# Seven half-size products in place of eight in a feed-forward down projection

## The chip, the cores and the metric

The kernel runs on one core of one Trainium2 chip. Its metric is the device time in microseconds. Three runs of the kernel before gave 2230.1 us in the median (2228.79 to 2231.28). TensorE, VectorE, ScalarE and GpSimd each have their own in-order queue of instructions and wait for each other by semaphores; SyncE issues the DMAs that load weights.

## The reference

The reference is two transformer blocks on 512 tokens of width 1024 in float32: attention, a gated delta rule and a mixture of experts, then a second block with an mLSTM, a short convolution and stick-breaking attention. The change touches only the second block's feed-forward part, whose width is 4096, and what follows it:

```
h2 = rmsnorm(x, norm_mlp_g)
x = x + square(relu(h2 @ w_up)) @ w_down      # w_up 1024x4096, w_down 4096x1024
return rmsnorm(x, norm_final_g)
```

## The kernel before, in words

Every dense product is computed in fp32r with a split: each operand is the sum of a high half (a rounded copy, made by a cast on ScalarE) and a low half (the rest, made by a subtraction on VectorE), and three matmuls, high x high and the two mixed ones, stand for one product.

Dense work is a list of jobs (`add_job`, L157). A job has a piece of weights of 128x1024 numbers, half of a 1 MB load. The loads go through a ring of two buffers (`ringA`, L2167), `get` takes a loaded one, and `release` frees it and issues the next load (L132 to L139). `presplit` (L167) makes the high and low half of the weights into one of three `hl` buffers, two jobs ahead of the job that runs (`run_jobs`, L197, `look=2`). Then the job's matmuls are issued and its result is taken out of PSUM.

The up projection uses `fm` (L234): each load gives two jobs of 24 matmuls (8 blocks of the contraction x 3 terms) that write the 128 hidden units of the job for all 512 tokens into one PSUM bank. `ev_up` (L2152) takes it out: relu on ScalarE, square on VectorE, then the high and low halves of the result into `uT`, which has one buffer per quarter of the hidden width, two in turn. The down projection uses `tm` (L287): for one quarter (1024 hidden units) and one half of the 1024 output columns (`nh`), four jobs of 24 matmuls add into four PSUM banks, one for each 128 tokens, and `ev_res` (L2131) adds each bank to `x1`, the residual stream in SBUF, on VectorE. The very last half goes through `tm_whole` (L319), which finishes one token block after the other, so that the final norm of a block can run beside the matmuls of the next. The loop at L1689 interleaves: up of quarter 0, then up of quarter q+1 and down of quarter q.

In this stage six PSUM banks serve the accumulators (`pacc3`) and two a pool `psm3`, which only the norm ahead of the stage uses (L1795). The order of instructions within an engine's queue is written when the program is built, by a list scheduler that goes by its own model of durations and by program order; it is not changed at run time. GpSimd has no work in the feed-forward stage but four tiny operations of the final norm.

Of the kernel before, what the change touches and what calls it, by code (L numbers as in the profile page):

```python
# [10 lines left out]
F32 = mybir.dt.float32  # L11
F32R = mybir.dt.float32r
# [3 lines left out]
AF = mybir.ActivationFunctionType  # L16
OP = mybir.AluOpType
# [9 lines left out]
def drain(g):  # L27
    for _ in g:
        pass
# [52 lines left out]
class Kern:  # L82
# [84 lines left out]
    def presplit(self, upto):  # L167
        while self.jsplit < min(upto, self.jlimit):
            j = self.jobs[self.jsplit]
            if j[3] != "second":  # L170
                self.cur_raw = self.get()
            ring, raw = self.cur_raw
            src = j[0](raw)
            if j[1] == "fm":
                hl = self.hlp.tile([128, 2, 8, 128], F32R, name="hl_fm", tag="hl")
            elif j[1] == "whole":
                hi, lo = hl = j[5]()
            elif j[1] == "tm":
# [108 lines left out]
    def tm(self, src, c0, evac, hsrc, rows=1024, r0=0, k0=0, close=True):  # L287

        st = {}
        nu = rows // 512  # L290
        for u in range(nu):
            self.ld_tm(src, r0 + u * 512, c0)
            for m in range(2):
                def view(raw, m=m):
                    return raw.rearrange("p (k c) -> p k c", k=4)[:, 2 * m:2 * m + 2, :]

                def mm(hl, u=u, m=m):
                    h = hsrc()
                    first, last = (u == 0 and m == 0), (u == nu - 1 and m == 1)
                    if first:  # L300
                        st["ps"] = [self.pacc.tile([128, 512], F32, name="acc", tag=self.atag)
                                    for _ in range(4)]
                    for c in range(4):
                        ps = st["ps"][c]
                        n = 0
                        for kk in range(2):
                            k = k0 + u * 4 + m * 2 + kk
                            for a, b in ((0, 0), (1, 0), (0, 1)):
                                self.TE.matmul(ps, h[:, a, k, c * 128:(c + 1) * 128], hl[:, b, kk, :],  # L309
                                               start=(first and n == 0), stop=(last and n == 5))  # L310
                                n += 1
                        self.step += 1
                        if last:
                            evac(c, ps)
                        self.catch_up(False)
                        yield 1.3
                self.add_job(view, "tm", mm, "first" if m == 0 else "second")

    def tm_whole(self, src, c0, evac, hsrc, tile, r0=0):  # L319

# [1323 lines left out]
    def b2_loads(self):  # L1644
        A = self.A
# [27 lines left out]
        self.tm_whole(A["w_out_2"], 512, lambda c, ps: self.ev_mid(c, ps), lambda: self.yM,  # L1673
                      lambda: self.sc.tile([128, 2, 8, 512], F32R, name="whole", tag="yB"))

        def up(q):
            for j in range(4):
                self.fm(A["w_up_2"], 1024 * q + 256 * j,
                        [lambda ps, q=q, j=2 * j + m: self.ev_up(q, j, ps) for m in range(2)], lambda: self.hT4)

        def down(q):
            for nh in range(2):
                if q == 3 and nh == 1:
                    self.tm_whole(A["w_down_2"], 512, lambda c, ps: self.ev_res(c, 1, ps, True), lambda: self.uT[3],
                                  lambda: self.b2.tile([128, 2, 8, 512], F32R, name="whole", tag="hT"), r0=1024 * q)
                else:
                    self.tm(A["w_down_2"], nh * 512, lambda c, ps, nh=nh: self.ev_res(c, nh, ps),
                            lambda q=q: self.uT[q], r0=1024 * q)
        up(0)  # L1689
        for q in range(4):  # L1690
            if q < 3:
                up(q + 1)
            down(q)

    def split_y(self, y, src, j):

# [53 lines left out]
    def second_block(self):  # L1750
        tc, A = self.tc, self.A
# [59 lines left out]
        with tc.tile_pool(name="mlp", bufs=1, reuse_waits="tile") as mp:  # L1811
            self.mp = mp
            gf = mp.tile([128, 1024], F32, name="gf")
            self.GE.dma_start(gf, self.bcast_rows(A["norm_final_g_2"], 1024))
            self.gf = gf
            self.uT = {}
            drain(first)
            drain(self.run_jobs(55))
            drain(self.tail())
        PN.__exit__(None, None, None)  # L1820
        PC.__exit__(None, None, None)
# [327 lines left out]
        next(g)  # L2149
        self.defer(lambda: drain(g), 4)  # L2150

    def ev_up(self, q, j, ps):  # L2152
        mp = self.mp
        if j == 0:
            self.uT[q] = mp.tile([128, 2, 8, 512], F32R, name="uT", tag="uT", bufs=2)
        r = mp.tile([128, 512], F32, name="up_r", tag="up_r", bufs=2)
        self.SE.activation(r, ps, AF.Relu)
        self.VE.tensor_mul(r, r, r)
        self.split_y(self.uT[q], r, j)


@with_exitstack
# [47 lines left out]
```

## Time and profile before

| | |
|---|---|
| median of the runs | 2230.1 us |
| the profiled execution | 2224.39 us |
| its span, first to last instruction | 2222.6 us |
| mean granted TensorE clock | 0.989 of full speed |
| TensorE busy in the span | 94% |
| feed-forward stage | 1863 to 2213 us of the span |

The profile's busy times count an instruction from its start to its end, waits for a shared resource within it included. The granted clock is in parts of full speed, 1.00 for 2.4 GHz and 0.50 for 1.2 GHz. The rows on which the prediction rests stand in a section of their own below.

### The profile page before, as it was taken

How to read it: one execution, taken by the hardware profiler on the slowest of the kernel's cores; microseconds unless marked ns; L12 is line 12 of the kernel's file. 1: busy time of each engine (PE TensorE's matmuls, PEld its weight loads, DVE VectorE, ACT ScalarE, POOL GpSimd, SP SyncE). 2: the span in 40 equal slices, each digit the busy share in tenths (PEclk: the TensorE clock that was granted, in tenths of full speed). 3: DMA queues.
4: the chain of work that ended last, by engine and by line, in shares of the span. 5: the costliest groups of instructions: out<-in, count | busy, mean ns of one | idle time of the engine just before them, and what ended most of it. 6: DMA issues, size and time to landing. Idle time of an engine off the chain costs nothing.

```text
span 2222.6 us, 28293 instructions
## 1 busy us (share of the span) xinstructions
PE 2092.1 (94%) x11741; PEld 1610.7 (72%) x11741; DVE 1016.1 (46%) x1635; ACT 756.4 (34%) x1181; POOL 175.8 (8%) x202
## 2 busy tenths in 40 slices
PE   6989999999888888889999999999999999999998
PEld 4767787755444444468888888888888888888886
DVE  5579667521111113555555345555454444434433
ACT  3645543311111011036666234445222343323221
POOL 1020001011111110021221000000000000000000
PEclk9999999999999999989999999999999999999999
DMA  6212101999999999811121232222333232332322
GB/s 192 76 57 76 59 2 31 362 388 417 418 416 408 405 405 397 342 59 57 58 63 56 91 92 76 73 72 82 109 96 95 95 118 82 95 95 95 95 95 76
DMA packets 161431, 354.25 MB, mean 159 GB/s; under 512 B 16678, under 2 KB 116111, under 8 KB 136723
## 3 DMA queue, kind: packets, MB, share of 16 engines
q1 hardware_dynamic: 151395, 339.24, 42.0%
q0 software_dynamic: 8480, 7.91, 1.0%
q10 hardware_dynamic: 1424, 5.24, 0.6%
q8 instruction: 94, 1.54, 0.3%
q14 instruction: 38, 0.31, 0.0%
HBM read 352.86 MB, written 22.02 MB: 169 GB/s over the span
## 4 chain that ended last, share of the span: by engine, by line
PE 55%; DVE 1%; ACT 0%; issue 0%; DMA 0%; POOLq 0%; ACTq 0%
PE acc L259 38%; PE acc L309 8%; PE acc L336 2%; PE acc L218 2%; PE sb_o L1941 1%; PE sb_z L1922 1%; PE ml_s L2063 1%; PE ml_pn L2083 1%; PE pv L1840 0%; PE sb_z L1881 0%; PE sb_z L1926 0%; PE n_ps L447 0%; PE sb_z L1888 0%; PE ml_pd L2083 0%; PE sb_z L1930 0%
## 5 line engine op out<-in xcount | busy, mean ns | idle before, releaser
L259 PE MATMUL acc<-hT,hl_fm 128*128 128x512 f32 x3504 | 822.1, 393 | 2.1 <-DVE hl_fm L165 2.0
L259 PEld LDWEIGHTS acc<-hT,hl_fm 128*128 128x128 f32 x3504 | 655.0, 189 | 140.7 <-issue 3.8
L165 DVE TENSOR_TENSOR hl_fm<-rawA,hl_fm 128x1024 fp32r<-128x1024 f32 x174 | 215.4, 1238 | 139.9 <-ACT hl_fm L161 139.8
L161 ACT CAST hl_fm<-rawA 128x1024 fp32r<-128x1024 f32 x176 | 184.7, 1049 | 267.5 <-PE acc L259 199.4
L309 PE MATMUL acc<-hl_tm,uT 128*128 128x512 f32 x672 | 152.8, 389 | 0.0
L309 PEld LDWEIGHTS acc<-hl_tm,uT 128*128 128x128 f32 x672 | 126.1, 188 | 26.2
L1448 PE MATMUL gu<-rawB,XT 128*64 128x256 f32 x992 | 130.9, 382 | 13.5 <-DMA rawB<-in_expert_w_gate_dram 13.5
L1448 PEld LDWEIGHTS gu<-rawB,XT 128*64 128x64 f32 x992 | 83.7, 137 | 49.8 <-DMA rawB<-in_expert_w_gate_dram 17.2
L1480 ACT ACTIVATE obs<-dn_o,slots 128x512 f32<-128x512 f32 x52 | 35.8, 688 | 234.3 <-PE dn_o L1477 234.3
L1437 DVE TENSOR_TENSOR XT<-g_ps,g 128x512 f32<-128x512 f32 x64 | 41.6, 686 | 143.8 <-PE g_ps L1431 143.0
L165 DVE TENSOR_TENSOR hl_tm<-rawA,hl_tm 128x1024 fp32r<-128x1024 f32 x48 | 58.7, 1224 | 66.4 <-ACT hl_tm L161 66.3
L259 PE MATMUL acc<-yA,hl_fm 128*128 128x512 f32 x384 | 87.4, 389 | 0.0
L259 PEld LDWEIGHTS acc<-yA,hl_fm 128*128 128x128 f32 x384 | 72.1, 188 | 14.9
L161 ACT CAST hl_tm<-rawA 128x1024 fp32r<-128x1024 f32 x48 | 50.3, 1048 | 93.0 <-PE acc L309 84.5
L1477 PE MATMUL dn_o<-rawB,ht 128*64 128x512 f32 x256 | 73.4, 600 | 8.8 <-DVE ht L1463 6.7
L1448 PE MATMUL gu<-rawC,XT 128*64 128x256 f32 x448 | 68.8, 386 | 6.5 <-DMA rawC<-in_expert_w_gate_dram 6.5
L309 PE MATMUL acc<-hl_tm,hT 128*128 128x512 f32 x288 | 72.4, 404 | 0.0
L1448 PE MATMUL gu<-rawH,XT 128*64 128x256 f32 x352 | 60.0, 401 | 11.0 <-DMA rawH<-in_expert_w_gate_dram 11.0
L1463 DVE COPY ht<-h_ps 128x256 f32<-128x256 f32 x32 | 13.6, 424 | 123.3 <-PE h_ps L1461 123.3
L1452 ACT ACTIVATE sg<-gu 128x256 f32<-128x256 f32 x32 | 12.3, 384 | 149.9 <-PE gu L1448 149.9
L309 PEld LDWEIGHTS acc<-hl_tm,hT 128*128 128x128 f32 x288 | 54.3, 194 | 10.9
L1454 DVE TENSOR_TENSOR hd<-sg,gu 128x256 f32<-128x256 f32 x32 | 13.4, 420 | 100.2 <-ACT sg L1452 100.2
(513 smaller groups left out, 2905.0 us busy)
## 6 DMA issues: line engine op xcount, KB each, us to landing
rawA<-in_w_in_dram SPq DMA_DIRECT2D x66, 1024.0 KB
rawB<-in_expert_w_up_dram SPq DMA_DIRECT2D x33, 1024.0 KB
rawB<-in_expert_w_down_dram SPq DMA_DIRECT2D x32, 1024.0 KB
rawB<-in_expert_w_gate_dram SPq DMA_DIRECT2D x29, 1024.0 KB
rawC<-in_expert_w_down_dram SPq DMA_DIRECT2D x16, 1024.0 KB
rawA<-in_w_up_dram SPq DMA_DIRECT2D x16, 1024.0 KB
rawA<-in_w_down_dram SPq DMA_DIRECT2D x16, 1024.0 KB
rawC<-in_expert_w_gate_dram SPq DMA_DIRECT2D x14, 1024.0 KB
```

Of the source, the lines that this page charges most:

```text
L161: self.SE.copy(hi, src)
L165: self.VE.tensor_sub(lo, src, hi.bitcast(F32))
L218: self.TE.matmul(p[:, t:t + 256], j[4][:, a, k, :], h[:, b, k, t:t + 256], start=(t == 0 and i == 0), stop=(t > 0 and i == 23), skip_group ...
L259: self.TE.matmul(ps, hl[:, a, k, :], h[:, b, k, :], start=(n == 0), stop=(n == 23))
L309: self.TE.matmul(ps, h[:, a, k, c * 128:(c + 1) * 128], hl[:, b, kk, :], start=(first and n == 0), stop=(last and n == 5))
L336: self.TE.matmul(ps, h[:, a, k, c * 128:(c + 1) * 128], st["w"][:, b, k, :], start=(n == 0), stop=(n == 23))
L1437: self.VE.tensor_tensor(xt[:, 4 * b:4 * b + 4, :], ps, self.g2[:, 4 * b:4 * b + 4, None].to_broadcast([128, 4, 128]), op=OP.mult)
L1448: TE.matmul(pg[64 * e:64 * e + 64, m * 256:(m + 1) * 256], xt[:, k, 64 * e:64 * e + 64], w[2 * m + e][:, k * 256:(k + 1) * 256], start=(m ...
L1477: TE.matmul(po[64 * e:64 * e + 64, :], ht[:, j, 64 * e:64 * e + 64], w[e].rearrange("p (j c) -> p j c", j=2)[:, j, s], start=(j == 0), sto ...
L1480: SE.activation(ob[:, s], po, AF.Copy, scale=sl[:, 1:2])
L1922: TE.matmul(z[e][b][:, c:c + n], self.ntri, hl[:, a, f:f + n], start=False, stop=(i == 3 and a == 1), skip_group_check=True)
L1941: TE.matmul(po[o, 512 - n:512], v[:, i, o], aa[e][:, self.FLAT[i]:self.FLAT[i] + n], start=(i == 0), stop=(i == 3))
```

## The change

The first three quarters of the hidden width (3072 of 4096) are cut into six chunks of 512. In a chunk, the down product is 512 tokens x 512 hidden units times 512 x 1024 weights. It is treated as a 2x2 block product (halves of the tokens, of the hidden units, of the output columns) and computed with seven block products in place of eight, by the Winograd form of Strassen's scheme: four operands are plain blocks, the others are sums of blocks.

On the weight side, `seven` takes both 1 MB loads of a chunk at once and makes P5 = W12 - W11, P6 = W22 - P5, P7 = W22 - W12 (in place) and later P4 = W21 - P6 on GpSimd; the seven jobs, in the order P1, P6, P2, P5, P7, P3, P4, have 12 matmuls each. The high halves are casts on ScalarE as before; the low halves of P6, P7 and P4 are subtractions on GpSimd, the other four on VectorE. On the token side, `ev_forms` writes seven forms for each pair of hidden blocks: relu on ScalarE, square on GpSimd, four sums of 256 columns on VectorE, and high and low halves of all. On the result side, `sums` gives pairs of PSUM banks: P2 adds into the banks of P1, P3 into those of P5, P4 into those of P7, in each case after the first result has been read out by VectorE; P6 adds over all six chunks in the two banks of `psm3`. P1 is summed into an SBUF tile `g_sum`, which, with P6 added, is added to three of the four blocks of `x1` at the end, on GpSimd. The last quarter runs as before: eight up jobs, then `tm` and `tm_whole`.

```diff
@@ presplit
+            if j[1] == "seven":
+                j[4] = j[0]()
+                self.jsplit += 1
+                continue
@@ new
+    SEVEN = (("P1", 0), ("P6", 4), ("P2", 1), ("P5", 3), ("P7", 5), ("P3", 6), ("P4", 2))
+    def seven(self, src, r0, forms, st, evac):
+        VE, SE, GE = self.VE, self.SE, self.GE
+        for nh in range(2):
+            self.ld_tm(src, r0, nh * 512)
...
+        def part(name):
+            if name == "P1":
+                w["raw"] = [self.get() for _ in range(2)]
+                w["P1"], w["P2"] = halves(w["raw"][0][1])
+                w12, w["P3"] = halves(w["raw"][1][1])
+                w["P5"] = self.mp.tile([128, 2, 512], F32, name="w_t1", tag="w_t1")
+                w["P6"] = w["P4"] = self.mp.tile([128, 2, 512], F32, name="w_t2", tag="w_t2")
+                GE.tensor_tensor(w["P5"], w12, w["P1"], op=OP.subtract)
+                GE.tensor_tensor(w["P6"], w["P3"], w["P5"], op=OP.subtract)
+                GE.tensor_tensor(w12, w["P3"], w12, op=OP.subtract)
+                w["P7"] = w12
+            hl = self.hlp.tile([128, 2, 2, 512], F32R, name="hl_tm", tag="hl")
+            x = w[name]
+            SE.copy(hl[:, 0], x)
+            if name in ("P6", "P7", "P4"):
+                GE.tensor_tensor(hl[:, 1], x, hl[:, 0].bitcast(F32), op=OP.subtract)
+            else:
+                VE.tensor_sub(hl[:, 1], x, hl[:, 0].bitcast(F32))
+            if name == "P2":
+                GE.tensor_tensor(w["P4"], x, w["P4"], op=OP.subtract)
+            if name in ("P2", "P3"):
+                self.release(w["raw"][name == "P3"][0])
+            return hl
+        def mm(hl, name, f):
+            u = forms()
+            ps, start, stop = st(name)
+            for r in range(2):
+                n = 0
+                for k in range(2):
+                    for a, b in ((0, 0), (1, 0), (0, 1)):
+                        self.TE.matmul(ps[r], u[:, f, a, k, r * 128:(r + 1) * 128], hl[:, b, k, :],
+                                       start=(start and n == 0), stop=(stop and n == 5), skip_group_check=True)
...
+            evac(name, ps)
...
+    def sums(self, c, n):
+        def st(name):
+            if name == "P6":
+                if c == 0:
+                    self.p6 = [self.psm.tile([128, 512], F32, name="p6", tag="ps") for _ in range(2)]
+                return self.p6, c == 0, c == n - 1
+            b = dict(P2="P1", P3="P5", P4="P7").get(name, name)
+            if b == name:
+                banks[b] = [self.pacc.tile([128, 512], F32, name="acc", tag=self.atag) for _ in range(2)]
+            return banks[b], b == name, b != name
+        def add(t, nh, ps):
+            for r in range(2):
+                x = self.x1[:, 2 * t + r, nh * 512:nh * 512 + 512]
+                VE.tensor_add(x, ps[r], x)
...
+            if name == "P1":
+                for r in range(2):
+                    if c == 0:
+                        VE.tensor_copy(g[:, r], ps[r])
+                    else:
+                        VE.tensor_add(g[:, r], ps[r], g[:, r])
...
+                    for t, nh in ((0, 1), (1, 0), (1, 1)):
+                        x = self.x1[:, 2 * t:2 * t + 2, nh * 512:nh * 512 + 512]
+                        GE.tensor_tensor(x, x, g, op=OP.add)
@@ b2_loads
-        up(0)
-        for q in range(4):
-            if q < 3:
-                up(q + 1)
-            down(q)
+        n = 6
+        for c in range(n):
+            up(512 * c, 2, lambda j, ps, c=c: self.ev_forms(c, j, ps))
+            if c:
+                self.seven(A["w_down_2"], 512 * (c - 1), lambda c=c - 1: self.uF[c], *self.sums(c - 1, n))
+        up(512 * n, 4, lambda j, ps: self.ev_up(j, ps))
+        self.seven(A["w_down_2"], 512 * (n - 1), lambda: self.uF[n - 1], *self.sums(n - 1, n))
+        self.tm(A["w_down_2"], 0, lambda c, ps: self.ev_res(c, 0, ps), lambda: self.uT, r0=512 * n)
+        self.tm_whole(A["w_down_2"], 512, lambda c, ps: self.ev_res(c, 1, ps, True), lambda: self.uT,
+                      lambda: self.b2.tile([128, 2, 8, 512], F32R, name="whole", tag="hT"), r0=512 * n)
@@ new
+    def ev_forms(self, c, j, ps):
...
+        r = self.ur[j] = mp.tile([128, 512], F32, name="up_r", tag="up_r", bufs=4)
+        SE.activation(r, ps, AF.Relu)
+        self.GE.tensor_tensor(r, r, r, op=OP.mult)
+        if j < 2:
+            return
+        u, k = self.uF[c], j - 2
+        a1, a2, b1, b2 = (self.ur[i][:, h * 256:h * 256 + 256] for i in (j - 2, j) for h in range(2))
+        d = mp.tile([128, 4, 256], F32, name="up_s", tag="up_s", bufs=2)
+        VE.tensor_add(d[:, 0], a2, b2)
+        VE.tensor_sub(d[:, 1], d[:, 0], a1)
+        VE.tensor_sub(d[:, 2], a1, a2)
+        VE.tensor_sub(d[:, 3], b1, d[:, 1])
+        for f, x in ((slice(0, 1), a1[:, None, :]), (slice(1, 3), r.rearrange("p (h t) -> p h t", h=2)), (slice(3, 7), d)):
+            SE.copy(u[:, f, 0, k, :], x)
+            VE.tensor_sub(u[:, f, 1, k, :], x, u[:, f, 0, k, :].bitcast(F32))
```

## Rows read from the trace of the kernel before

**Rows 1.** The page, busy time, share of the span and instructions of each engine.
```profile
PE 2092.1 (94%) x11741; PEld 1610.7 (72%) x11741; DVE 1016.1 (46%) x1635; ACT 756.4 (34%) x1181; POOL 175.8 (8%) x202
```

**Rows 2.** Chain that ended last, 1850 us on: start us, us, engine, line.
```profile
1952.32 43.52 PE acc L309 x192
...
2191.68 21.77 PE acc L336 x96
```

**Rows 3.** Table by stretch, one up and one down quarter; its columns are the first row.
```profile
core 0: us, PE busy (x) PEld busy (x) DVE busy (x) ACT busy (x) POOL busy (x), PEclk, DMA share, GB/s
...
1995.80:2039.40 43.60, 43.60 (x194) 36.10 (x193) 19.55 (x23) 15.43 (x22) 0.00 (x0) 1.00 0.29 95
2039.40:2082.90 43.50, 43.50 (x193) 36.03 (x192) 15.56 (x17) 9.44 (x10) 0.00 (x0) 1.00 0.31 99
```

**Rows 4.** Groups by line, 1880 us on: busy us, mean ns, idle before.
```profile
L165 DVE TENSOR_TENSOR hl_tm<-rawA,hl_tm 128x1024 fp32r<-128x1024 f32 x28 | 34.3, 1225 | 59.4 <-ACT hl_tm L161 59.4
L161 ACT CAST hl_tm<-rawA 128x1024 fp32r<-128x1024 f32 x28 | 29.4, 1051 | 76.0 <-PE acc L309 76.0
...
L1698 DVE TENSOR_TENSOR uT<-up_r,uT 128x512 fp32r<-128x512 f32 x32 | 21.9, 684 | 0.7 <-ACT uT L1697 0.7
L2133 DVE TENSOR_TENSOR x<-acc,x 128x512 f32<-128x512 f32 x32 | 21.5, 688 | 20.8 <-PE acc L309 12.1 <-PE acc L336 8.7
L2158 DVE TENSOR_TENSOR up_r<-up_r 128x512 f32<-128x512 f32 x31 | 21.5, 693 | 78.5 <-ACT up_r L2157 78.5
...
L2157 ACT ACTIVATE up_r<-acc 128x512 f32<-128x512 f32 x31 | 18.6, 598 | 98.3 <-PE acc L259 98.3
```

**Rows 5.** Groups by line on GpSimd, whole span.
```profile
L2096 POOL TENSOR_TENSOR ml_P<-ml_P 128x512 f32<-128x512 f32 x4 | 5.2, 1297 | 298.6 <-ACT ml_P L2095 298.6
...
L163 POOL TENSOR_TENSOR hl_fm<-rawA,hl_fm 128x1024 fp32r<-128x1024 f32 x2 | 4.7, 2353 | 0.6 <-ACT hl_fm L161 0.6
```

**Rows 6.** Groups by line on VectorE, whole span: a 256-wide subtraction.
```profile
L165 DVE TENSOR_TENSOR ml_Ps<-ml_P,ml_Ps 128x256 fp32r<-128x256 f32 x4 | 1.7, 426 | 1.9 <-ACT ml_Ps L161 1.9
```

**Rows 7.** Timeline around 965 us: start us, us, engine, line, operation.
```profile
964.96 2.35 POOL L163 TENSOR_TENSOR hl_fm<-rawA,hl_fm 128x1024 fp32r<-128x1024 f32 x1 [0.59 <-ACT hl_fm L161]
...
965.14 3.25 DVE L442 SCALAR_TENSOR_TENSOR n_xn<-x,rs_n,g_mix 128x1024 f32<-128x1024 f32 x1
...
968.31 1.27 DVE L451 TENSOR_TENSOR hT<-n_ps,hT 128x512 fp32r<-128x512 f32 x2
...
968.77 2.35 POOL L163 TENSOR_TENSOR hl_fm<-rawA,hl_fm 128x1024 fp32r<-128x1024 f32 x1
```

**Rows 8.** Groups by line on VectorE, whole span: the norm operation of rows 7 elsewhere.
```profile
L442 DVE SCALAR_TENSOR_TENSOR n_xn<-x,rs_n,g_mlp 128x1024 f32<-128x1024 f32 x4 | 5.1, 1283 | 2.7 <-POOL rs_n L424 2.7
```

**Rows 9.** Timelines of GpSimd and of VectorE around 993 us.
```profile
992.13 0.61 POOL L1865 CAST sb_K<-sb_k 64x512 fp32r<-64x512 f32 x1 [18.47 <-ACT sb_k L1834]
992.80 2.27 POOL L1866 CAST sb_K<-sb_k 64x512 fp32r<-64x512 f32 x1
...
992.77 0.69 DVE L1868 TENSOR_TENSOR sb_Kl<-sb_k,sb_K 64x512 fp32r<-64x512 f32 x1 [1.53 <-POOL sb_K L1865]
993.38 1.21 DVE L165 TENSOR_TENSOR hl_fm<-rawA,hl_fm 128x1024 fp32r<-128x1024 f32 x1
```

**Rows 10.** Timeline of the tail: two weight loads issued, the casts that waited for them.
```profile
2166.86 10.18 SPq L152 DMA_DIRECT2D rawA<-in_w_down_dram  x2
...
2173.20 2.00 ACT L161 CAST whole<-rawA 128x1024 fp32r<-128x1024 f32 x2 [2.19 <-DMA rawA<-in_w_down_dram]
...
2181.56 2.00 ACT L161 CAST whole<-rawA 128x1024 fp32r<-128x1024 f32 x2 [5.11 <-DMA rawA<-in_w_down_dram]
```

**Rows 11.** Timeline of TensorE and table by stretch around 968 us.
```profile
968.44 1.97 PE L447 MATMUL n_ps<-ident,n_xn 128*128 128x128 f32 x8 [3.34 <-DVE n_xn L442]
...
965.00:970.00 5.00, 1.66 (x9) 1.56 (x8) 4.59 (x5) 2.20 (x4) 5.00 (x3) 0.71 0.00 0
970.00:972.00 2.00, 1.85 (x8) 1.34 (x8) 1.62 (x3) 1.73 (x5) 1.12 (x1) 0.50 0.00 0
```

More of the change, by code (lines that the diff above doesn't have):

```diff
@@ L317, in tm, with halves @@
                 self.add_job(view, "tm", mm, "first" if m == 0 else "second")
+    SEVEN = (("P1", 0), ("P6", 4), ("P2", 1), ("P5", 3), ("P7", 5), ("P3", 6), ("P4", 2))
[3 more added lines that the diff above has]
+            self.ld_tm(src, r0, nh * 512)
+        w = {}
+        def halves(t):
+            v = t.rearrange("p (k c) -> p k c", k=4)
+            return v[:, 0:2, :], v[:, 2:4, :]
+        def part(name):
[30 more added lines that the diff above has]
+                                       start=(start and n == 0), stop=(stop and n == 5), skip_group_check=True)
+                        n += 1
+                self.step += 1
+                self.catch_up(False)
+                yield 1.3
+            evac(name, ps)
+        for name, f in self.SEVEN:
+            self.jobs.append([lambda name=name: part(name), "seven",
+                              lambda hl, name=name, f=f: mm(hl, name, f), "only", None, None])
@@ new lines, in sums, with evac @@
+    def sums(self, c, n):
+        VE, GE = self.VE, self.GE
+        banks = {}
+        def st(name):
[11 more added lines that the diff above has]
+                VE.tensor_add(x, ps[r], x)
+        def evac(name, ps):
+            g = self.mp.tile([128, 2, 512], F32, name="g_sum", tag="g_sum") if c == 0 and name == "P1" else None
+            if g is not None:
+                self.gsum = g
+            g = self.gsum
+            if name == "P1":
[4 more added lines that the diff above has]
+                        VE.tensor_add(g[:, r], ps[r], g[:, r])
+            elif name == "P2":
+                add(0, 0, ps)
+            elif name in ("P5", "P7"):
+                add(1, 1, ps)
+            elif name == "P3":
+                add(0, 1, ps)
+            elif name == "P4":
+                add(1, 0, ps)
+                if c == n - 1:
+                    for r in range(2):
+                        VE.tensor_add(g[:, r], self.p6[r], g[:, r])
+                    for t, nh in ((0, 1), (1, 0), (1, 1)):
+                        x = self.x1[:, 2 * t:2 * t + 2, nh * 512:nh * 512 + 512]
+                        GE.tensor_tensor(x, x, g, op=OP.add)
+        return st, evac
@@ L1674, in b2_loads, with up @@
                       lambda: self.sc.tile([128, 2, 8, 512], F32R, name="whole", tag="yB"))
[L1676 to L1688, printed above, removed]
-        up(0)
-        for q in range(4):
-            if q < 3:
-                up(q + 1)
-            down(q)
+        def up(c0, n, ev):
+            for j in range(n):
+                self.fm(A["w_up_2"], c0 + 256 * j, [lambda ps, j=2 * j + m: ev(j, ps) for m in range(2)], lambda: self.hT4)
+        n = 6
[8 more added lines that the diff above has]
+                      lambda: self.b2.tile([128, 2, 8, 512], F32R, name="whole", tag="hT"), r0=512 * n)
     def split_y(self, y, src, j):
@@ L1815, in second_block @@
             self.gf = gf
-            self.uT = {}
+            self.uF, self.ur = {}, {}
             drain(first)
-            drain(self.run_jobs(55))
+            drain(self.run_jobs(len(self.jobs) - self.jptr - 6))
             drain(self.tail())
@@ L2150, in ev_mid, with ev_up @@
         self.defer(lambda: drain(g), 4)
-    def ev_up(self, q, j, ps):
+    def ev_up(self, j, ps):
         mp = self.mp
         if j == 0:
-            self.uT[q] = mp.tile([128, 2, 8, 512], F32R, name="uT", tag="uT", bufs=2)
-        r = mp.tile([128, 512], F32, name="up_r", tag="up_r", bufs=2)
+            self.uT = mp.tile([128, 2, 8, 512], F32R, name="uT", tag="uT", bufs=2)
+        r = mp.tile([128, 512], F32, name="up_r", tag="up_r", bufs=4)
         self.SE.activation(r, ps, AF.Relu)
         self.VE.tensor_mul(r, r, r)
-        self.split_y(self.uT[q], r, j)
+        self.split_y(self.uT, r, j)
+    def ev_forms(self, c, j, ps):
+        mp, VE, SE = self.mp, self.VE, self.SE
+        if j == 0:
+            t = mp.tile([128, 2, 8, 512], F32R, name="uT", tag="uT", bufs=2)
+            self.uF[c] = t.rearrange("p a k t -> p (a k t)")[:, 0:7168].rearrange("p (f a k t) -> p f a k t", f=7, a=2, k=2)
+        r = self.ur[j] = mp.tile([128, 512], F32, name="up_r", tag="up_r", bufs=4)
[13 more added lines that the diff above has]
+            VE.tensor_sub(u[:, f, 1, k, :], x, u[:, f, 0, k, :].bitcast(F32))
 @with_exitstack
```

## The prediction

> **What bounds the kernel now.** I read the page's engine line first: TensorE is busy 94% of the span, VectorE 46%, ScalarE 34%, GpSimd 8% [rows 1]. Then the chain that ended last, over the feed-forward part: it is matmuls one behind the other from 1863 us to 2213 us, 192 down matmuls in 43.52 us, so 0.2267 us each, with no piece of another engine in between [rows 2]. The table by stretch says the same of an up and of a down quarter: TensorE fills them, at full clock, VectorE is busy 19.55 and 15.56 us of some 43.5, and GpSimd does nothing at all [rows 3]. So a matmul that goes is worth 0.2267 us, as long as the other engines stay ahead. What they do in the stage is in the groups by line: per weight half a ScalarE cast of 1.05 us and a VectorE subtraction of 1.225 us, and 0.69 us for each result added out of PSUM [rows 4].
>
> **What the change removes.** Six chunks of 512 contraction rows go from 8 block products to 7. A product of half size is 2 row blocks x 2 k blocks x 3 split terms = 12 matmuls of the same 128x512 form, so a chunk has 84 instead of 96, and the kernel 72 fewer: 72 x 0.2267 = 16.3 us. Each of the five middle chunks now has 96 up and 84 down matmuls on TensorE, 40.8 us where it had 43.5. The last up quarter and the last down quarter stay as they were. If everything else is hidden, this is the whole effect.
>
> **What it adds, per middle chunk.** GpSimd: three weight sums, a fourth (P4), and the low halves of P6, P7 and P4, all 128x1024 with two inputs in SBUF. The trace has that form twice, 2.353 us each, so 7 x 2.353 = 16.5 us. The four squares, 128x512, cost 1.297 us each by the GpSimd addition of that shape, 5.2 us [rows 5]. Together 21.7 us.
> VectorE, with both inputs in SBUF: eight low halves (four up, and P1, P2, P5, P3) x 1.225 = 9.8 us [rows 4]; the token forms, twice per chunk four 256-wide sums and low halves of 256, 512 and 1024 columns. The 256-wide row is 0.426 us [rows 6], so 2 x (5 x 0.43 + 0.68 + 1.225) = 8.1 us. With one input in PSUM: twelve additions x 0.688 = 8.3 us [rows 4]. Together 26.2 us.
> ScalarE: eleven casts of 1.05, four relus of about 0.6, and form casts of some 2.2 us twice: about 18 us. It has room.
> By share alone each engine fits into 40.8 us. They do not fit independently, which decides this case.
>
> **The cost that a busy share does not show.** Where the norm of the second block runs, a GpSimd subtraction with both inputs in SBUF starts at 964.96 and ends at 967.31; a VectorE operation with two SBUF inputs that starts at 965.14 is recorded with 3.25 us, that is to 968.39 [rows 7]. The same VectorE operation in the feed-forward norm takes 1.283 us [rows 8]. It stood still until GpSimd was done and then ran. Beside the second such GpSimd subtraction VectorE does two operations with one input in PSUM and one in SBUF: 1.27 us for both, against 0.69 for one in the stage, so nothing is lost [rows 4, 7]. The other direction is in the trace too: a GpSimd cast of 64x512 that takes 0.61 us takes 2.27 us when VectorE has two subtractions back to back, 0.69 and 1.21 us, at that moment; it waited out both [rows 9]. So GpSimd and VectorE's two-SBUF-input work take turns, instruction by instruction. I price the change as if they shared one server: 21.7 + 9.8 + 8.1 = 39.6 of 40.8 us per chunk. VectorE's PSUM additions may run under GpSimd, but they sit in the same in-order queue behind blocked subtractions.
>
> The Trainium skill has this as a rule ("SBUF — State Buffer", section "Who interferes with whom"): a VectorE instruction with two SBUF inputs contends with a GpSimd instruction that reads SBUF, and whoever issues second waits until the first is finished. The trace agrees on the standstill (3.25 for 1.28 us). On turns it says more: by issue order alone the GpSimd cast would have waited for one VectorE instruction, and it waited for two [rows 9]. What strict first-come turns would make of the time is the third rival below.
>
> **Where in a chunk it does not fit.** Let a chunk begin at 0 with its first up job. An up job takes 5.44 us, a product 2.72; P1 starts at 21.8, P6 at 24.5, P2 at 27.2, and P4 ends at 40.8. A ring of two buffers holds the weights: the chunk's second down buffer is the one the third and fourth up jobs used, free when the fourth's low half is made, about 5.4 + 1.05 + 1.225 = 7.7. The load lands 4.5 to 6.3 us later, as the two loads of the tail do [rows 10], at about 13. Before that no sum can start. From 13 to 40.8, in 27.7 us, the shared path has to carry: on GpSimd the seven 128x1024 operations and two squares, 16.5 + 2.6 = 19.1; on VectorE the lows of P2, P5, P3 and of the next two up jobs, 5 x 1.225 = 6.1, and both sets of forms, 8.1. Sum 33.3 us, 5.6 too many. Ten of the twelve PSUM additions fall in the same window, 6.9 us. P2 may not start before VectorE has taken P1's result out of the bank, P3 not before P5's, P4 not before P7's, so a late VectorE holds TensorE directly, with only the one product between them, 2.72 us, as cover.
> Lower end: the forms are needed only a chunk later; if they drift into the next up phase, where the path is nearly empty, 33.3 - 8.1 = 25.2 fits and nothing is lost. Upper end: no addition hides, 5.6 + 6.9 = 12.5 us. I take half of the additions hidden, as they can run only under a GpSimd operation and not when a blocked subtraction stands ahead of them: 5.6 + 3.45 = 9.0 us lost per chunk.
> The sixth chunk follows eight plain up jobs and its squares and forms are elsewhere: GpSimd 16.5, VectorE 3.7 + 2.5 for lows and 2 x 1.37 for the last two up results, 25.4 in the 27.7, so it fits. The three last corrections of x on GpSimd, 7.1 us, lie under the 21.8 us of the next plain product. What follows the last matmul is untouched.
>
> **Sum.** -16.3 + 5 x 9.0 = +28.7 us. The profiled execution took 2224.39 us, span 2222.6; that gives 2253 for such an execution. It lies 5.7 us under the median of the runs, 2230.1, on which I state the forecast: 2230.1 + 28.7 = 2259. Break-even is 3.3 us lost per chunk.
>
> **Clock.** TensorE idle for 3.34 us before 968.44, after an earlier pause, and the granted clock is 0.71 over 965 to 970 and 0.50 in the next 2 us [rows 11]: 1.2 GHz instead of 2.4. In the feed-forward stage it is 1.00 [rows 3]. With 9 us of waits per chunk in pieces of 1 to 5 us a fall is possible; a TensorE that runs slow while it would wait anyhow costs nothing, so I take 0 and keep up to 3 us per chunk, +15, for the range.
>
> **Rivals.**
> 1. The path fits (faster). The order that the scheduler writes lets the forms slip into the up phase and GpSimd work under the PSUM additions; TensorE stays the bound. For it: 39.6 is under 40.8, and a whole up phase stands ready for work that may come late. Against it: an order fixed at build time meets these standstills at run time, and 97% of a shared path leaves no room for a wait. Time: 2230.1 - 16.3 + 0 to 5 = 2214 to 2219. Chance 0.18.
> 2. Part of it fits: the forms of one of two pairs slip, 5.6 + 3.45 - 4.05 = 5 lost, less what the sums can gain when the load lands early; 3 to 4 us per chunk, 2230.1 - 16.3 + 15 to 20 = 2229 to 2234, no change that can be told. Chance 0.08.
> 3. GpSimd takes its turn each time, VectorE's queue stands behind 2.35 us pieces and no addition is hidden: 12.5 per chunk, 2230.1 - 16.3 + 62.5 = 2276, with the clock up to 2291. Chance 0.16.
> 4. The loads are the bound: each chunk needs both ring buffers for the sums. Without any standstill the chain is 13, sums to 20, the second square 1.3, low of P6 to 23.7, against its need at 25: a landing 1.2 us later than I took costs nothing, the slowest of the tail's costs under 1 us. 2214 to 2220; its chance, 0.03, is inside rival 1's.
> The forecast itself, 5 to 11 us lost per chunk, 2239 to 2269: 0.58.
>
> **Numbers.** What a measurement of this kernel tells from no change is about 0.2%, 4.5 us. Faster: rival 1, with a little of 2: 0.19. Same: 0.08. Slower: the forecast and rival 3, 0.73. The likeliest case alone has 2239 to 2269; to hold 8 in 10 the range goes down into rival 1 and up into rival 3: 2217 to 2284.
>
> **What would show it.** Right: about 72 fewer matmuls; VectorE subtractions of 128x1024 recorded with 2 to 4 us instead of 1.225 in the seven-product stretches, and GpSimd's 128x1024 operations with more than 2.353; TensorE waiting for VectorE ahead of P2 or P7 and for GpSimd's lows ahead of P6 or P4, some 9 us per middle chunk and near 0 in the sixth. Wrong: those operations at their old durations, or standstills that leave TensorE busy throughout; then the time is rival 1's. If TensorE waits for loads, or falls to half clock for most of the stage, the size has another cause than mine.

## The result and the profile after

The changed kernel takes 2270.99 us in the median of four runs (2269.14 to 2271.29), the kernel before beside it 2229.44 us (2224.26 to 2231.28). The ratio is 1.0181, 95% interval 1.0165 to 1.0198: slower by 41.5 us. That is inside the range of the prediction (2217 to 2284) and 2 us above its likeliest case (2239 to 2269). The profiled execution took 2270.85 us, its span is 2269.1 us, its mean granted clock 0.975.

The engine line of the page, against [rows 1], says that the work itself came out as planned:

```profile
PE 2101.5 (93%) x11669; PEld 1610.8 (71%) x11669; DVE 1096.9 (48%) x1721; ACT 786.2 (35%) x1211; POOL 323.2 (14%) x271
```

TensorE has 72 instructions fewer (11741 to 11669), yet is busy 9 us longer: matmuls that ran at a lower clock. GpSimd has 147 us more.

The table by stretch of the changed kernel (columns as in [rows 3]): the first two middle chunks, the sixth, and then pieces of the third, from the matmuls of P1 and P6 on.

```profile
1893.80:1947.06 53.26, 44.49 (x182) 35.35 (x181) 34.64 (x40) 20.19 (x25) 24.04 (x12) 0.90 0.25 80
1947.06:1998.26 51.20, 44.22 (x182) 35.56 (x181) 28.68 (x35) 17.45 (x21) 23.16 (x11) 0.90 0.26 83
2151.86:2216.70 64.84, 63.48 (x278) 51.57 (x277) 43.51 (x41) 23.91 (x31) 21.12 (x8) 1.00 0.30 98
2020.00:2025.46 5.46, 5.46 (x25) 4.17 (x23) 5.03 (x2) 0.62 (x1) 5.21 (x3) 1.00 0.00 0
2025.46:2031.29 5.83, 0.01 (x1) 0.04 (x1) 3.79 (x8) 3.65 (x5) 1.58 (x1) 0.76 0.00 0
2031.29:2033.60 2.31, 1.19 (x3) 0.47 (x3) 2.31 (x5) 1.54 (x3) 0.00 (x0) 0.50 0.00 0
2033.60:2037.00 3.40, 3.40 (x8) 2.72 (x9) 3.40 (x3) 0.83 (x1) 2.49 (x1) 0.50 0.58 157
```

A middle chunk should take 40.8 us (180 x 0.2267, [rows 2]); it takes 53.3 the first time and 51.2 afterwards. TensorE stands still for 5.83 us after P6, gets two matmuls in, stands still again for 1.12, and does the next matmuls at a granted clock of 0.50, so that its 180 matmuls are busy for 44.2 us. The excess of the five chunks is 12.5, 10.4, 10.4, 10.5 and 10.4 us, that of the sixth 2.3 (64.84 against 276 x 0.2267 = 62.6): 56.3 us. Less the 16.3 us of the 72 matmuls that is 40.0. From the first up matmul to the last down matmul (called the stage from here on) the traces give 350.0 us before and 390.0 after: the same 40.0. Nothing moved elsewhere.

What TensorE waited for, in the list of waits over 1880 to 2270 us (total us, times, longest):

```profile
PE acc L372 <- DVE g_sum L413: 23.5, 4, 5.9
PE acc L372 <- DVE hl_tm L357: 7.0, 7, 1.1
PE acc L372 <- DVE g_sum L411: 5.9, 1, 5.9
PE p L372 <- POOL hl_tm L355: 1.7, 1, 1.7
```

Five times, once per middle chunk, P2 waits about 5.9 us until VectorE has read P1's bank into `g_sum` (L411 in the first chunk, L413 later). The rest is VectorE's low half L357. GpSimd itself is waited for only 1.7 us.

The chain of waits through the third chunk, in order of time (start us, us, what), shows how the delay builds up:

```profile
1998.26 8.82 PE acc L263 x39
2007.08 4.96 DMA rawA<-in_w_down_dram
...
2012.16 2.39 POOL w_t L347
...
2016.98 2.42 POOL rawA L349
2019.40 1.01 POOL up_r L2277
...
2020.43 2.60 DVE up_s L2283
2023.04 2.54 DVE up_s L2285
2025.58 0.33 DVE up_s L2284
2025.91 0.60 DVE uT L2289
2026.51 0.34 DVE up_s L2286
...
2026.88 1.04 ACT uT L2288
2027.92 0.51 ACT up_r L2276
...
2028.50 1.59 POOL up_r L2277
...
2030.11 0.42 DVE up_s L2283
2030.54 0.60 DVE g_sum L413
...
2033.60 15.82 PE acc L372 x58
```

TensorE is on it for 24.6 of the 51 us only. The weights land at 2012.05, 13.8 us into the chunk. Three sums follow on GpSimd, then, in the same queue, the square of the third up result, with which the first pair of hidden blocks is complete. VectorE's first two sums of forms then take 2.60 and 2.54 us where the third, a like operation, takes 0.33 of the chain: GpSimd is busy in just that time with P6's low half and P4's sum. Then the queues pass the delay on: ScalarE's next relu, of the fourth up result, stands behind the cast that waits for these forms, the next square behind the relu, the second forms behind the square, and the reading of P1's bank behind the first of those.

Turn by turn this is seen in the timelines of the same chunk. GpSimd (start us, us, operation, idle time before it in brackets):

```profile
2020.34 2.41 POOL L355 TENSOR_TENSOR hl_tm<-w_t,hl_tm 128x1024 fp32r<-128x1024 f32 x1
2022.83 2.46 POOL L360 TENSOR_TENSOR w_t<-rawA,w_t 128x1024 f32<-128x1024 f32 x1
...
2034.51 3.00 POOL L355 TENSOR_TENSOR hl_tm<-rawA,hl_tm 128x1024 fp32r<-128x1024 f32 x1 [4.43 <-ACT hl_tm L353]
```

and VectorE:

```profile
2020.43 2.60 DVE L2283 TENSOR_TENSOR up_s<-up_r 128x256 f32<-128x256 f32 x1 [8.13 <-POOL up_r L2277]
2022.96 2.62 DVE L2285 TENSOR_TENSOR up_s<-up_r 128x256 f32<-128x256 f32 x1
2025.50 0.41 DVE L2284 TENSOR_TENSOR up_s<-up_s,up_r 128x256 f32<-128x256 f32 x1
...
2034.06 1.22 DVE L2289 TENSOR_TENSOR uT<-up_s,uT 128x1024 fp32r<-128x1024 f32 x1
2035.19 3.40 DVE L357 TENSOR_TENSOR hl_tm<-w_t,hl_tm 128x1024 fp32r<-128x1024 f32 x1
```

Each VectorE operation that starts inside a GpSimd operation ends some 0.3 us after it: 0.41 us of work, recorded with 2.6. At 2034.51 it is GpSimd's turn to be second: it waits out L2289 (to 2035.28) and is recorded with 3.00; VectorE's next, L357, then waits out GpSimd (to 2037.51) and is recorded with 3.40.

The groups by line over 1880 to 2270 us, against [rows 4, 5] (busy us, mean ns, idle before):

```profile
L357 DVE TENSOR_TENSOR hl_tm<-w_t,hl_tm 128x1024 fp32r<-128x1024 f32 x6 | 13.3, 2212 | 0.0
L355 POOL TENSOR_TENSOR hl_tm<-rawA,hl_tm 128x1024 fp32r<-128x1024 f32 x6 | 21.2, 3530 | 23.3 <-ACT hl_tm L353 23.3
L401 DVE TENSOR_TENSOR x<-acc,x 128x512 f32<-128x512 f32 x60 | 39.5, 684 | 10.3 <-PE acc L372 10.2
```

P5's low half, made on VectorE, takes 2.21 us in the mean where a low half took 1.225, and P7's, on GpSimd, 3.53 instead of 2.353. These two meet in every chunk; the other 18 low halves of L357 are recorded with 1.315 us in the mean, the other twelve of L355 with 2.440. Which of the two goes first differs: in the first and third chunk it is GpSimd (3.00 and 3.40 us, as above), in the second, fourth and fifth VectorE, whose L357 keeps 1.22 while GpSimd waits through two operations:

```profile
1983.36 4.13 POOL L355 TENSOR_TENSOR hl_tm<-rawA,hl_tm 128x1024 fp32r<-128x1024 f32 x1 [4.43 <-ACT hl_tm L353]
```

The additions out of PSUM keep their 0.68: one input outside SBUF, and no standstill.

### The profile page after: what moved, and what is told of

It is laid out like the page before. It is cut to its first block, busy times and chain, and to the rows that moved or that the text cites. A ratio compares the mean times of both kernels' runs of the same rounds, so it can differ in the third digit from the quotient of the medians.

```text
span 2269.1 us, 28408 instructions
## 1 busy us (share of the span) xinstructions
PE 2101.5 (93%) x11669; PEld 1610.8 (71%) x11669; DVE 1096.9 (48%) x1721; ACT 786.2 (35%) x1211; POOL 323.2 (14%) x271
## 4 chain that ended last, share of the span: by engine, by line
PE 50%; DVE 3%; POOL 2%; DMA 1%; issue 1%; ACT 1%; POOLq 0%; ACTq 0%; DVEq 0%
PE acc L263 34%; PE acc L372 4%; PE acc L448 2%; PE acc L313 2%; PE acc L222 2%; DMA rawA<-in_w_down_dram 1%; PE sb_o L2049 1%; PE sb_z L2030 1%; DVE up_s L2283 1%; PE ml_s L2171 1%; PE ml_pn L2191 1%; POOL up_r L2277 1%; DVE up_s L2285 1%; POOL rawA L349 1%; POOL w_t L347 1%
## 5 line engine op out<-in xcount | busy, mean ns | idle before, releaser
L372 PE MATMUL acc<-hl_tm,uT 128*128 128x512 f32 x432 | 116.9, 431 | 36.4 <-DVE g_sum L413 23.5
L372 PEld LDWEIGHTS acc<-hl_tm,uT 128*128 128x128 f32 x432 | 89.4, 210 | 62.7 <-ACT uT L2288 31.4
L1651 POOL DMA_INDIRECT yd<-obs,dest x26 | 26.3, 1010 | 331.7 <-ACT obs L1592 331.7
L536 POOL TENSOR_TENSOR rs_n<-rs_n,mhalf 128x1 f32<-128x1 f32 x12 | 9.5, 791 | 372.5 <-DVE rs_n L535 372.5
```

The lines of the kernel that those rows point to most:

```text
L372: self.TE.matmul(ps[r], u[:, f, a, k, r * 128:(r + 1) * 128], hl[:, b, k, :], start=(start and n == 0), stop=(stop and n == 5), skip_group ...
L1651: self.GE.indirect_dma_start(out=self.yd[:, :], out_offset=bass.IndirectOffsetOnAxis(ap=self.dest[:, r:r + 1], axis=0), in_=ob, in_offset= ...
```

## The experiments

Theory: GpSimd and VectorE's work with two SBUF inputs share one path, and VectorE's delays hold TensorE ahead of P2. Rivals: the order of the queues alone (squares behind sums, relus behind casts), with every operation at its own length; and the clock, half speed after each wait. Single runs differ by a few us outside the stage, so the stage's length stands beside the time. The kernel before took 2229.53 us on the chip of the first four runs, 2226.12 on that of the next three (e5 to e7), 2228.94 on that of the last four (e8 to e11).

**e1: the squares on ScalarE.**

```diff
-        self.GE.tensor_tensor(r, r, r, op=OP.mult)
+        SE.activation(r, r, AF.Square)
```

> One edit to the changed kernel: the squares of the hidden units in the six chunks are made by ScalarE (Square, in place) and no longer by GpSimd. Shared path (my theory): 2.6 of the 33.3 us that the path must carry in a chunk's window go, so some 2 to 3 us of the 7 us that TensorE waits per middle chunk go: 2252 to 2262. Queue order (rival): the squares stand on GpSimd behind three weight sums, the forms behind the squares, and the reading of P1's bank behind the forms; with the squares off GpSimd the wait ahead of P2 goes with no regard to the path: 2214 to 2230. Clock (rival): nothing changes unless the waits shrink below what lets the clock fall.

2249.75 us, stage 369.1. This takes the squares, 4 x 1.24 us per chunk, off the path and out of GpSimd's queue, and gives back 21 of the 41 us: far from the value of the queue order, 2 us better than the path's range. TensorE now waits about 3.1 us ahead of P2 instead of 5.9. The squares no longer stand behind GpSimd's sums, but two-input operations of VectorE are still long (three of the four 256-wide sums 1.27 to 1.42 us in the mean). The chain of waits of one chunk has these, one behind the other:

```profile
2009.40 2.53 DVE up_s L2285
2011.93 2.53 DVE up_s L2284
```

At its own length each takes 0.34 of a chain, and L2283 ahead of them took 1.00 instead of 0.34: 5.0 us of standstills on the way to P2, more than TensorE waits there. So the order of the queues does not explain what is left in e1, and the standstills do.

**e2: GpSimd writes instead of computing, equally long.** Every sum, low half and square of GpSimd becomes fills of the same tiles (two of 128x1024 and one half for 2.4 us, two of 128x512 for a square). Nothing is read. The fills also wait for less than the operations in their place: a low half's for no high half, and those of P5's and P6's tiles for no weights.

```diff
-                GE.tensor_tensor(w["P5"], w12, w["P1"], op=OP.subtract)
...
+                for t in (w12, w["P5"], w["P5"][:, 0]):
+                    GE.memset(t, 0.5)
```

> GpSimd's work in the chunks is replaced by fills of about the same length that read nothing: two and a half fills of 1024 columns for each weight sum and low half, two of 512 for each square (so the weight sums, these low halves and the squares are left out of the computation). GpSimd stays as busy and its results as late; only its reads of SBUF are gone. Shared path: VectorE's 128x1024 subtractions are back at 1.225 us and TensorE's waits all but vanish: 2212 to 2225. Queue order: the waits stay, 2250 to 2271. A low half may start before its high half here, which can flatter this run by 1 us or so per chunk.

2210.18 us, stage 334.3. The table by stretch of one middle chunk of this kernel:

```profile
1970.98:2011.78 40.80, 40.80 (x182) 33.78 (x181) 23.91 (x35) 17.37 (x21) 20.58 (x29) 1.00 0.33 103
```

and its groups by line, 1890 to 2160 us:

```profile
L359 POOL MEMSET hl_tm<- 128x1024 f32 x36 | 34.4, 956 | 30.7 <-PE p L377 19.2 <-PE acc L377 10.8
L361 DVE TENSOR_TENSOR hl_tm<-rawA,hl_tm 128x1024 fp32r<-128x1024 f32 x18 | 22.0, 1220 | 17.8 <-ACT hl_tm L356 17.8
```

GpSimd is busy 20.6 us per chunk, nearly as long as in the change, and TensorE has no gap: 40.80 of 40.80, at full clock. VectorE's low half is back at 1.220 us. So it is not GpSimd's busy time by itself that costs. The order of the queues is not excluded by this run, though, as GpSimd's timeline shows (the fill of `w_t` is that of the next chunk's P5; P6's follows at 2005.59):

```profile
1985.21 2.55 POOL L352 MEMSET rawA<- 128x1024 f32 x3
...
2000.16 0.96 POOL L348 MEMSET w_t<- 128x1024 f32 x1
```

The fills of P5's and P6's tiles thus run during the products of the chunk before. Between the landing and the first square only 3.6 us of fills for the sums are left, where the change has 7.2 us of sums, and the square behind them is through 19.5 us into the chunk and not 22.1. In VectorE's queue, written at build time, one addition to `g_sum` and P2's low half stand further ahead than in the change. e2 shows that fills do not delay VectorE; it does not show that the order costs nothing.

**e3: no GpSimd in the chunks.** Squares on ScalarE; sums and all low halves on VectorE.

```diff
-                GE.tensor_tensor(w["P5"], w12, w["P1"], op=OP.subtract)
+                VE.tensor_sub(w["P5"], w12, w["P1"])
...
-            if name in ("P6", "P7", "P4"):
-                GE.tensor_tensor(hl[:, 1], x, hl[:, 0].bitcast(F32), op=OP.subtract)
-            else:
-                VE.tensor_sub(hl[:, 1], x, hl[:, 0].bitcast(F32))
+            VE.tensor_sub(hl[:, 1], x, hl[:, 0].bitcast(F32))
```

> Nothing on GpSimd in the chunks: squares on ScalarE, weight sums and all low halves on VectorE, everything else as in the changed kernel. VectorE then has 26.2 + 4 x 1.225 + 3 x 1.225 = 34.8 us of work per chunk of 40.8. Shared path: no standstill is left, TensorE is the bound again, 2212 to 2222, faster than before by 8 to 18 us. Queue order: about the same, as sums of 1.2 us end 3.5 us sooner. Rival against both: VectorE at 85% is late in the products, and TensorE waits 3 us or more per chunk: 2229 and above.

2213.41 us in the median of six runs (2211.18 to 2216.38), stage 333.7; ratio to the kernel before 0.9932, 95% interval 0.9918 to 0.9947. One middle chunk in the table by stretch:

```profile
1972.01:2012.81 40.80, 40.80 (x182) 33.78 (x181) 31.57 (x42) 19.50 (x25) 0.00 (x0) 1.00 0.32 103
```

With more work on VectorE (31.6 us instead of 28.7) and none on GpSimd, TensorE is never late. 16.1 us are gained over the kernel before, where the 72 matmuls are worth 16.3: this version beats both, and it is the change without its offload. Both explanations foresaw that; what it excludes is a VectorE that is too full.

**e4: useless matmuls in TensorE's pause**, 24 behind P6 in each chunk, to keep the clock up.

```diff
+            if name == "P6":
+                d = self.pacc.tile([128, 512], F32, name="fill", tag=self.atag)
+                for i in range(24):
+                    self.TE.matmul(d, u[:, f, 0, 0, 0:128], hl[:, 0, 0, :], start=(i == 0), stop=(i == 23))
```

> The changed kernel with 24 useless matmuls behind P6 in each chunk, 5.4 us of TensorE work, in the place of the wait of 5.8 us ahead of P2 (they write a bank that nobody reads). Clock: the engine no longer stands still long enough for the clock to fall, the 3.4 us per middle chunk that half clock costs come back: 2250 to 2258. If the slow stretch only covers waits that would be there anyhow: 2268 to 2275. If the 24 matmuls do not fit into the wait, each chunk is up to 5.4 us longer: up to 2298.

2271.31 us, stage 391.3: nothing gained. Two chunks in its table by stretch:

```profile
1997.94:2049.09 51.15, 47.15 (x206) 38.06 (x205) 30.59 (x35) 17.47 (x21) 22.10 (x11) 1.00 0.27 83
2049.09:2098.03 48.94, 46.93 (x205) 38.05 (x205) 29.31 (x35) 17.48 (x21) 23.38 (x11) 1.00 0.28 86
```

The clock is 1.00 in these two, and they take 51.15 and 48.94 us, against 51.2 at 0.90. At full speed TensorE runs into the next wait instead: the time that it waits for VectorE's L357 grows from 7.0 to 12.5 us. The slow matmuls had been covering waits. The four later middle chunks are 0 to 2.3 us shorter each, 3.2 together, and not the 3.4 each that the busy time suggests; the first is 1.3 and the sixth, which had no such pause, 3.2 us longer.

**e5 and e6: useless GpSimd work beside e3**, whose result nobody reads: multiplications of `x1` and `g_sum` in e5, fills of the same length in e6.

```diff
+                t, nh = dict(P2=(0, 0), P3=(0, 1), P4=(1, 0), P7=(1, 1)).get(name, (0, 0))
+                y = self.x1[:, 2 * t:2 * t + 2, nh * 512:nh * 512 + 512] if name != "P1" else self.gsum
+                for _ in range(2):
+                    GE.tensor_tensor(d, y, y, op=OP.mult)        # e5
+                    GE.tensor_copy(d[:, 0, 0:1], y[:, 0, 0:1])   # e6, and then fills:
+                    for z in (d, d, d[:, 0]):
+                        GE.memset(z, 0.5)
```

> The version without GpSimd (squares on ScalarE, sums and lows on VectorE, 2213) with useless work on GpSimd in five of the six chunks: two multiplications of 128x1024 from SBUF behind each of P1, P2, P7, P3 and P4, ten per chunk, some 24 us, into a scratch tile that nobody reads. No result of GpSimd is waited for, so lateness of its results plays no part. Shared path: VectorE has 26.5 us of two-input work per chunk, with 24 us of GpSimd 50 in 40.8 us, nearly all in the stretch of the products; it stands still again, 3 to 9 us per chunk: 2228 to 2258, and its subtractions are recorded with over 2 us. Queue order: no change, 2210 to 2217.

> The same as the run with idle reads, at the same places and about as long (each multiplication replaced by fills of 1024, 1024 and 512 columns and a copy of one column that keeps the place), but without reading SBUF. Shared path: no standstill, 2210 to 2217. If any work of GpSimd beside VectorE costs, read or not: as slow as the run with idle reads.

2251.74 and 2233.68 us, stages 373.8 and 353.1. e6 misses what was expected, and the waits show why: in both kernels VectorE's next addition to x waits until GpSimd has read it, 20 us in total. So neither isolates the path; only their difference, 18 us, speaks for it. They were mended in e8 and e9.

**e7, e10, e11: one part of GpSimd's work put back into e3**: the four weight sums (e7), the squares (e10), the three low halves (e11), each by the changed kernel's own lines.

```diff
-                VE.tensor_sub(w["P5"], w12, w["P1"])
+                GE.tensor_tensor(w["P5"], w12, w["P1"], op=OP.subtract)
...
-        SE.activation(r, r, AF.Square)
+        self.GE.tensor_tensor(r, r, r, op=OP.mult)
...
+            if name in ("P6", "P7", "P4"):
+                GE.tensor_tensor(hl[:, 1], x, hl[:, 0].bitcast(F32), op=OP.subtract)
```

> The version without GpSimd, but the four weight sums of a chunk back on GpSimd, 9.6 us, as the change has it; lows and squares stay off it. Shared path: three of the sums fall between the landing of the weights and P1, where VectorE has little two-input work, the fourth into the products; 26.5 - 4.9 + 9.6 = 31 of 40.8 us, a loss of 0 to 4 us per chunk: 2213 to 2234, so the sums alone are the smaller part of the 40 us. Queue order: the sums start with the landing as late as in the changed kernel and P6 waits for them, 2 us and more per chunk: 2224 and above.

> The version without GpSimd, with the squares alone back on GpSimd, four of 1.04 us per chunk. Shared path: 4.2 us more on a path that carries 26.5 of 40.8; 0 to 1.5 us per chunk: 2211 to 2221.

> The version without GpSimd, with the low halves of P6, P7 and P4 alone back on GpSimd, 7.2 us per chunk, all among the products where VectorE is fullest. Shared path: each may hold VectorE for up to 2.35 us; 1 to 4 us per chunk: 2218 to 2233. With the sums alone (2237) and the squares alone, the three parts should add up to less than the 57 us between the change and the version without GpSimd, as waits overlap, or to more if they push each other.

| | us | stage us | over e3's stage |
|---|---|---|---|
| e7, sums | 2236.95 | 356.7 | 23.0 |
| e10, squares | 2220.94 | 340.8 | 7.1 |
| e11, lows | 2217.06 | 341.8 | 8.1 |
| the change, all three | 2270.99 | 390.0 | 56.3 |

The sums alone undo the gain; they are the part with three GpSimd operations back to back. The parts add up to 38.2 us, all together cost 56.3; that each delays the others is the likely reason, not shown. e7 lies above what the path was thought to cost and in the range of the queue order. Its chain through the chunk from 1982.6 us has 3.4 us of standstills, a low half of 2.33 instead of 1.13 us and one of the forms' of 2.80 instead of 0.60, out of the 4.6 us that a chunk lost. e10 lies inside its range, e11 1 us under.

**e8 and e9: e5 and e6 mended.** GpSimd reads a constant tile; a copy of one column pins the place.

```diff
+                v = self.gf.rearrange("p (r c) -> p r c", r=2)
...
+                GE.tensor_copy(d[:, 0, 0:1], y)
+                for _ in range(2):
+                    GE.tensor_tensor(d, v, v, op=OP.mult)   # e8
+                    for z in (d, d, d[:, 0]):               # e9
+                        GE.memset(z, 0.5)
```

> The idle reads once more, mended: in the two runs before, VectorE's additions to x waited for GpSimd's reading of x. Now GpSimd multiplies a constant tile by itself into a scratch tile, ten times 128x1024 per chunk, each pair behind a copy of one column that fixes its place; nobody waits for any of it. Shared path: VectorE's two-input work stands still behind it, 3 to 6 us per chunk: 2228 to 2243. Any other reason: 2210 to 2217.

> As the run before, with fills of the same length in the place of the multiplications, so GpSimd is as busy and reads nothing but the single columns. Shared path: 2210 to 2217. If GpSimd's work costs without reading too: as slow as the mended idle reads.

2248.66 and 2213.47 us, stages 363.2 and 333.7. Groups by line of e8, 1890 to 2160 us:

```profile
L409 POOL TENSOR_TENSOR idle<-gf 128x1024 f32<-128x1024 f32 x60 | 140.1, 2334 | 4.8
L165 DVE TENSOR_TENSOR hl_fm<-rawA,hl_fm 128x1024 fp32r<-128x1024 f32 x27 | 49.9, 1848 | 18.3 <-ACT hl_fm L161 18.1
L354 DVE TENSOR_TENSOR hl_tm<-rawA,hl_tm 128x1024 fp32r<-128x1024 f32 x20 | 40.3, 2013 | 6.1 <-ACT hl_tm L353 5.9
L398 DVE TENSOR_TENSOR x<-acc,x 128x512 f32<-128x512 f32 x50 | 31.9, 676 | 0.0
```

and of e9:

```profile
L410 POOL MEMSET idle<- 128x1024 f32 x120 | 114.7, 956 | 7.0
L165 DVE TENSOR_TENSOR hl_fm<-rawA,hl_fm 128x1024 fp32r<-128x1024 f32 x26 | 31.7, 1220 | 21.0 <-ACT hl_fm L161 20.4
L354 DVE TENSOR_TENSOR hl_tm<-rawA,hl_tm 128x1024 fp32r<-128x1024 f32 x24 | 29.2, 1216 | 17.6 <-ACT hl_tm L353 17.6
```

The rows count 60 multiplications, twelve per chunk in five chunks and not ten, and that is the number to read the result by; 60 sets of fills stand against them, 2.44 us each instead of 2.33. VectorE's queue has the same order in both but for one low half per chunk, which stands one place earlier in e9. Nobody waits for the multiplications, and the stage is 29.5 us longer: 5.9 per chunk, at the upper end of what was expected, though the time lies 6 us above its range. VectorE's low halves take 1.85 to 2.01 us in the mean, the additions out of PSUM keep 0.68. Beside the fills VectorE runs at 1.22 and the stage is e3's to 0.1 us. That is the theory by itself: reading on GpSimd delays VectorE and costs time although no result of it is waited for, writing does not. The Trainium skill ("SBUF — State Buffer", section "Who interferes with whom") says the same of a GpSimd instruction that only writes: such a VectorE instruction does not contend with it.

The mean of 2.33 us is a mix. Three rows of e8 show it, two of GpSimd and one of VectorE:

```profile
1990.95 1.89 POOL L409 TENSOR_TENSOR idle<-gf 128x1024 f32<-128x1024 f32 x1
1992.92 2.75 POOL L409 TENSOR_TENSOR idle<-gf 128x1024 f32<-128x1024 f32 x1
1992.08 1.85 DVE L165 TENSOR_TENSOR hl_fm<-rawA,hl_fm 128x1024 fp32r<-128x1024 f32 x1
```

The first multiplication, which waits for nobody, takes 1.89 us. VectorE's low half stands still until that is done, at 1992.84, and ends 1.08 us later; the second multiplication waits for the low half and takes 2.75.

## Why the prediction was right, and by how much it was off

The forecast was 2259, 12 us low, and the measured 2271 lies nearer to the third rival's 2276. The sign and the place held, and of the mechanism the larger part; that the loss per chunk came near the sum is partly luck.

- **72 matmuls, -16.3 us.** Right: 72 fewer instructions, 40.80 us per chunk in e2 and e3, 16.1 us gained in e3.
- **One shared path.** Right as a mechanism. P5's low half takes 2.2 instead of 1.22 us and P7's 3.5 instead of 2.35, as they meet, and two sums of forms per chunk 2.6 instead of 0.41; e2 and e9 show that it is GpSimd's reading, e8 that it costs although nothing depends on it. The Trainium skill's rule ("SBUF — State Buffer", section "Who interferes with whom": the second to issue waits for the first) agrees with the pairs at 2020 us, 2.60 us for 0.41 of work. In e8 the turns are whole ones, too. Who comes next is not settled by who issued first: GpSimd waited through two VectorE operations in [rows 9] and in three of the five middle chunks (4.13 us), through one in the other two (3.00).
- **Loss per middle chunk, 9.0 us.** The term that was mis-sized: 12.5 in the first and 10.4 in the other four, 54.1 against 45. The sum of shares (5.6 us too many in the 27.7 us window, and half of 6.9) named the right order of size for another reason than it gave, which is luck: the PSUM additions keep their 0.68 us and hardly count. What sets the end is a serial chain: load at 13.8 (13 was assumed), three sums, then the square that stood ready for 4 us behind them, two standstills of VectorE of 2.2 us each, and the fourth up result held up in ScalarE's and GpSimd's queues until the first forms were through. Part of that chain needs no standstill. GpSimd, at its own length throughout, is through P4's sum at 2025.29; with the next square (1.06), the first form (0.34) and the addition to `g_sum` (0.60) behind it, P1's bank is read at 2027.3, 1.9 us after P6. Followed on to P2's low half, this estimate leaves some 3.8 of the 6.95 us that TensorE waits in the chunk to the order of the queues alone. e1, where the squares are out of that order, is in keeping with this: it gives back 20.9 us of the stage, about 4 per middle chunk (though the squares are off the path as well), and keeps 35.4 over e3's.
- **The wait's place.** Ahead of P2 for VectorE, as said, 5.9 us in each middle chunk. Ahead of P7 nothing of note, and GpSimd's low halves ahead of P6 and P4, named too, hardly made TensorE wait: 1.7 us once.
- **Sixth chunk, 0.** It lost 2.3 us: the two-input squares and low halves of its last up jobs met GpSimd as well. Together with the 9.1 us of the middle chunks this is 11.4 of the 12 us.
- **Squares at 1.297 us.** Too dear: the one at 2019.34 us, which nothing delayed, is recorded with 1.06, the mean with delays is 1.242. It reads one tile twice; the row of [rows 5] that it was priced by is another operation of that shape.
- **Clock, 0.** A chunk's mean clock of 0.90 is 0.10 x 51.2 / 0.5 = 10 us at half speed, pauses included, and its matmuls are busy 3.4 us longer, a little above the upper bound of 3. In e4 keeping the clock up saves 0 to 2.3 us in a later middle chunk, so that the price of nothing was near.
- **Rivals.** That the path fits (1) and that the loads bind (4) are excluded by 5.9 us of waiting for VectorE, that part of it fits (2) by a loss of 10.4 us and not 3 to 4; the load does stand at the head of the chain, though. Rival 3, 2276, has the first chunk's 12.5 us exactly and the later ones' not, and its pieces of 2.35 us are in the chain: GpSimd does take its turn ahead of both sums of forms.

What stays open: how the 10.4 us split exactly. The standstills are on the chain and cost by themselves (e1, e8), and the order of the queues adds to them; its share of some 4 us is an estimate and a difference between two kernels of unlike orders. A kernel with the change's exact order and no reads on GpSimd was not run, as e2 moved part of the fills.

## What to carry to other kernels

Work with two SBUF inputs that goes to GpSimd beside a VectorE with such work of its own is not parallel: it takes 2.35 instead of 1.22 us and delays the rest, so count both as one queue and first ask whether VectorE could do it all (31.6 of 40.8 us here, with nothing lost). Let ScalarE take what has one input, such as a square. Where standstills threaten, price the chain through one period of the loop and not the shares, since a late operation holds whatever stands behind it in its queue.

## What the runs showed of the hardware

GpSimd's fills leave VectorE untouched: 1.216 to 1.220 us in e9, with 146 us of fills in 270 us. The turns are whole ones: in e8 a multiplication on GpSimd takes 1.89 us alone and 2.75 behind a low half. Their order is not fixed: GpSimd's low half of P7 waited through one VectorE operation in two middle chunks (3.00 us) and through two in three (4.13). A delayed TensorE at half clock can cost little or nothing: a chunk took 51.15 us at clock 1.00, another 48.94, against 51.2 at 0.90, as the slow matmuls ran in time that would have been waited.
